# A hybrid attention and convolution layer on one core: the DRAM scratch of v and q laid out for two load transfers a head

## The chip, the core and the metric

The kernel runs on one core of a Trainium2 chip. A core has a matrix engine (TensorE, PE in the profile, its weight loads as PEld), a vector engine (VectorE, DVE), a scalar engine (ScalarE, ACT), GpSimd (POOL), an engine that here only issues transfers (SyncE, SP) and 16 DMA engines that move data between DRAM and the on-chip memory. Engines run side by side; each takes its own instructions in order and waits where data isn't there yet. A transfer is issued by an instruction in the queue of SP, ACT or POOL. The metric is the device time of one execution in microseconds (us); lower is better.

## The reference

One layer over 1024 latent tokens (16 rows of 64) of width 1024, with 256 context tokens.

```python
h  = rmsnorm(x, norm_g) * (1 + scale) + shift          # adaLN from c; hc likewise from ctx
q, k, v, za, u, bg, cg, zc = split(h @ w_in)           # 8 x 512 columns
kc, vc = split(hc @ w_in[:, 512:1536])
q, k, kc = rmsnorm per head (8 heads of 64)
s_lat = rope(q) . rope(k) / 8 + bias, in an 8 x 16 window; s_ctx = q . kc / 8
p = softmax over both;  attn = (p_lat . v + p_ctx . vc) * silu(za)
conv = bg * conv3(cg * u) * silu(zc)
out = x + gate * (concat(attn, conv) @ w_out)
```

Everything is float32. Products of full precision are made from a high and a low part of each factor, so q, k, v and the weights each exist twice.

## The kernel before

The work has four stages. First the conditioning, the normalised and transposed tokens and the first convolution group. Then the projections of q, k and v (the loop at line 1161): four pairs of heads, eight token tiles of 128 each. Then the attention (line 1284): 8 heads in four quarters each, 32 quarters and a tail, with the matmuls of the remaining columns of `w_in` as fillers between a quarter's parts. Last the output projection (from line 1311).

On-chip memory doesn't hold q, k and v of all heads, so the projections write them to scratch in DRAM and the attention loads a head at a time.

- Writing: `spill` (203) keeps stores in a list that `flush` (1157) sends to SP's queue once per tile. `turn_qk` (226) writes, for two token tiles at a time, q (`q_d`, line 243: for each head a store for the high and one for the low part, each with rotated and plain q) and k (`k_d`). Line 1209 writes v of two token tiles (`v_d`), `turn_kc` (269) the context's k and v (`kc_d`, `vc_d`, 279 and 280).
- Reading, class `head` (927): `load_k` (935) two transfers of 512 KB; `load_q` (941) four of 256 KB for q, two of 128 KB for the context's k; `load_v` (951) for high and low part four of 64 KB, each with two blocks of v, and one of 64 KB with the context's two blocks, ten in all; `masks` (960) one of 576 KB with the bias. In DRAM `q_d` is [high or low, 64, pair of tiles, rotated or plain, 256] and `v_d` [128, pair of tiles, high or low, 128]. On the chip v of a head is `[128, 2, 10, 65]`: eight blocks of v and two of the context, 64 columns each and a column that sums the weights; there are two such tiles (`vts`, 1249), and head h uses the one of head h - 2.

The order in the attention: PE, DVE, ACT and POOL keep the program's order (class `ordered`, 44; `strict`, 1279). SP is not among them there, so the scheduler places its transfers, and neither are the transfers that ACT issues: `ordered` leaves `dma_start` of the other engines alone. The loop (1284) asks for v of head h at its first quarter, for bias, q and the context's k of head h + 1 at its second and for k of head h + 1 at its third.

A quarter n (`quarter`, 1057) does the scores of two blocks (`scores`, 983, into `pss`) and of 256 queries against the context (`ctx_scores`, into `pc`, copied to `sc` by ACT), the maxima (`mx`, then transposed on PE as `pmx`, reduced to `rm`, spread and copied by ACT to `mg`) and exponentials (`phc`, `plc`, `phl`, `pll`) of quarter n - 2, and the products with v (`ctx_out`, `lat_out`, into `po`) of quarter n - 3. In `finish` (1029) ACT copies half a finished head to `ob` and issues two stores from its own queue, the sums (`rs_d`, 1033) and the output (`o_d`, 1034). The fillers load their weights as `uraw` (`unit_load`, 291, on SP) and ACT casts them to `uh`; each filler unit's SiLU is stored to `zs_d` (495) by SP. `gated` (1257) multiplies finished pairs with that.

```python
        def put():
            ...
                for l in range(2):
                    spill(q_d[h][l, :, t0 // 2], qs[rows, l])
    ...
    def load_v(self):
        ...
        for l in range(2):
            for t in range(4):
                sp.dma_start(self.v[:, l, 2 * t:2 * t + 2, 0:HD]..., v_d[h][:, t, l]...)
            sp.dma_start(self.v[:, l, NB:, 0:HD]..., vc_d[h][:, l]...)
```

Of the kernel before, what the change touches and what calls it, by code (L numbers as in the profile page):

```python
# [10 lines left out]
F32 = mybir.dt.float32  # L11
# [8 lines left out]
P = 128  # L20
D = 1024
T = 1024
# [3 lines left out]
NB = 8  # L26
NH, HD = 8, 64
# [12 lines left out]
def body(tc, es, x, ctxt, w_ada, b_ada, w_in, q_g, k_g, rpbr, w_out, vecs, cst, out):  # L40
# [22 lines left out]
    sp = ordered(nc.sync)  # L63
# [26 lines left out]
    def many(name, n, shape):  # L90
        return [dr.tile(shape, F32, name=f"{name}{i}")[:] for i in range(n)]
# [9 lines left out]
    zs_d = many("zs_d", NPAIR, [P, T])  # L101


    q_d = many("q_d", NH, [2, HD, 4, 2, 256])
    k_d = many("k_d", NH, [HD, 4, 2, 256])
    v_d = many("v_d", NH, [P, 4, 2, 2 * HD])
    kc_d = many("kc_d", NH, [HD, 2, L])
    vc_d = many("vc_d", NH, [P, 2, 2 * HD])
    ri_d = many("ri_d", NPAIR, [2, T])


# [48 lines left out]
    def chunk_load(col, k):  # L160
        raw = wpp.tile([P, 3, P], F32, name="wr", tag="wr", bufs=5)
        chunk_anchor[:] = [sp.dma_start(raw, bass.AP(w_in.tensor, w_in.offset + (k * P) * 4096 + col,
                                                     [[4096, P], [512, 3], [1, P]]))]
        return raw
# [23 lines left out]
    def halves(dst, lo, src):  # L188
        act.copy(dst, src)
        dve.tensor_tensor(lo, src, dst.bitcast(F32), ALU.subtract)  # L190

    def put_v(vs, i, ps):

        halves(vs[:, :, 0, i], vs[:, :, 1, i], ps.rearrange("p (s d) -> p s d", s=2))
# [8 lines left out]
    def spill(dst, src):  # L203
        stores.append(lambda: sp.dma_start(dst, src.bitcast(F32)))
# [21 lines left out]
    def turn_qk(pp, p, two, t0):  # L226

        pA = psm.tile([P, 2, 2, P], F32, name="trA", tag="C", bufs=2)
        pB = psm.tile([P, 512], F32, name="trB", tag="C", bufs=2)
        for i, (qn, rot) in enumerate(two):  # L230
            pe.transpose(pA[:, 0, i], rot[:, 0:P], ident)
            pe.transpose(pA[:, 1, i], qn[:, 0:P], ident)
            pe.transpose(pB[:, i * P:(i + 1) * P], rot[:, P:256], ident)

        def put():
            qs = pp.tile([P, 2, 2, 256], F32R, name="qs", tag="qs", bufs=2)
            halves(qs[:, 0], qs[:, 1], pA[:].rearrange("p k i d -> p k (i d)"))
            ks = pp.tile([P, 2, 256], F32R, name="ks", tag="ks", bufs=2)
            halves(ks[:, 0], ks[:, 1], pB[:, :256])
            for s in range(2):  # L240
                h, rows = 2 * p + s, slice(64 * s, 64 * s + 64)
                for l in range(2):
                    spill(q_d[h][l, :, t0 // 2], qs[rows, l])
                spill(k_d[h][:, t0 // 2], ks[rows])
        return put

# [22 lines left out]
    def turn_kc(pp, p, two, vs):  # L269
        pB = psm.tile([P, 512], F32, name="trC", tag="C", bufs=2)  # L270
        for i in range(2):
            pe.transpose(pB[:, i * P:(i + 1) * P], two[i], ident)

        def put():
            ks = pp.tile([P, 2, 256], F32R, name="ks", tag="ks", bufs=2)
            halves(ks[:, 0], ks[:, 1], pB[:, :256])
            for s in range(2):
                h, rows = 2 * p + s, slice(64 * s, 64 * s + 64)
                spill(kc_d[h], ks[rows])
                spill(vc_d[h], vs[:, s].rearrange("p l i d -> p l (i d)"))  # L280
        return put

    def proj_tile(ch, t):
        ps = bank("pacc", "OOSS"[t % 4])
        for k in range(KT):
            wh, wl = ch[k]
            mm3(ps[:, :384], hh[k][:, t * P:(t + 1) * P], hl[k][:, t * P:(t + 1) * P], wh, wl, k == 0, k == KT - 1)
        return ps


    def unit_load(col):
        raws = []
        for q in range(2):
            raws.append(uw.tile([P, 4, P], F32, name="uraw", tag="uraw", bufs=2))
            sp.dma_start(raws[q], w_in[0, q * 512:(q + 1) * 512, col:col + P].rearrange("(k p) n -> p k n", p=P))
        return raws
# [84 lines left out]
    def z_col(f):  # L381
        return CZA + f * P if f < 4 else CZC + (f - 4) * P
# [407 lines left out]
    for m in range(1, 4):  # L790
        k, new, last = 2 * m, m < 3, m == 3
# [135 lines left out]
    class head:  # L927
# [13 lines left out]
        def load_q(self):  # L941
            h = self.h
            self.q = self.place().tile([P, 2, T], F32R, name="q_s", tag="B")
            self.kc = bmp.tile([P, 2, L], F32R, name="kc_s", tag="kc_s", bufs=2)
            for i in range(2):
                rows = slice(64 * i, 64 * i + 64)
                for k in range(2):
                    sp.dma_start(self.q[rows, k].bitcast(F32).rearrange("p (t c) -> p t c", c=256), q_d[h][i, :, :, k])
                sp.dma_start(self.kc[rows].bitcast(F32), kc_d[h])

        def load_v(self):
            h = self.h
            self.v = vts[h % 2]
            for l in range(2):
                for t in range(4):
                    sp.dma_start(self.v[:, l, 2 * t:2 * t + 2, 0:HD].bitcast(F32),
                                 v_d[h][:, t, l].rearrange("p (b d) -> p b d", d=HD))
                sp.dma_start(self.v[:, l, NB:, 0:HD].bitcast(F32), vc_d[h][:, l].rearrange("p (b d) -> p b d", d=HD))

        def masks(self):  # L960
            self.bt = bmp.tile([P, 3, 384], F32, name="bt", tag="bt", bufs=2)
# [195 lines left out]
    def flush():  # L1157
        while stores:
            stores.pop(0)()

    for n in range(NT + 3):


        p, t = divmod(n, NB)
        at = 2 if p < NPAIR - 1 else 0
        if 1 <= t and p + 1 < NPAIR:
            raws += [chunk_load(CQ + (p + 1) * P, k) for k in ([t - 1] if t < NB - 1 else [t - 1, t])]
        if n == 0:
            loaded[z_col(4)] = unit_load(z_col(4))
        if n == NT - 8:  # L1170
            loaded[z_col(0)] = unit_load(z_col(0))
        if 1 <= n <= KT:
            gate.load(n - 1)
        if 9 <= n < 25 and n % 2:
            next(tables)
        if n == NT - 6:
            heads[0].masks()
            heads[0].load_k()
        if n == NT - 5:
            heads[0].load_q()  # L1180
        flush()

        if t == 0 and 0 < n < NT:
            nxt += map(chunk_split, raws)
            ch, nxt, raws = nxt, [], []
        if n == 0:
            next(group0)
        if n == NT - 4:
            next(fill)
        if n < NT:  # L1190
            tiles[n] = proj_tile(ch, t)
        else:
            for _ in range((4, 3, 1)[n - NT]):
                next(fill)
        if 5 <= n < 9:
            for _ in range(2):
                next(group0)
        if n == 9:
            for _ in group0:
                pass  # L1200
        if 0 < n <= NT:
            scales[n - 1] = head_scale(pp, tiles[n - 1], 4)
            if n % 2:
                vs = pp.tile([P, 2, 2, 2, HD], F32R, name="vs", tag="vs", bufs=4)
            put_v(vs, (n - 1) % 2, tiles[n - 1][:, 256:384])
            if n % 2 == 0:
                q, r = divmod(n - 1, NB)
                for s in range(2):
                    spill(v_d[2 * q + s][:, r // 2], vs[:, s].rearrange("p l i d -> p l (i d)"))
        if t == at + 1 and n < NT:  # L1210
            cscales = [head_scale(pp, a, 2) for a in cacc]

        if 1 < n <= NT + 1:
            m, r = n - 2, (n - 2) % NB
            qn = rms_normed(pp, tiles[m], scales.pop(m))
        while waiting:
            waiting.pop(0)()
        if 4 <= t and p + 1 < NPAIR:
            nxt.append(chunk_split(raws.pop(0)))
        if 1 < n <= NT + 1:  # L1220
            tiles[m] = rotated(pp, rope, qn, r)
        if t == at + 2 and n < NT:
            kc = normed_ctx(pp, cacc, cscales)
        do_dves()
        if 2 <= n < KT + 2:
            gate.add(n - 2)
        if 9 <= n < 25 and n % 2 == 0:
            next(tables)
        do_acts()

        if n == KT + 5:
            gate.sum()
        if t == at and n < NT:
            cacc = ctx_products(ch)
        if n % 2 == 0 and n >= 4:
            waiting.append(turn_qk(pp, (n - 4) // NB, [tiles.pop(n - 4), tiles.pop(n - 3)], (n - 4) % NB))
        if t == at + 3 and n < NT:
            waiting.append(turn_kc(pp, p, *kc))
# [38 lines left out]
    with sbuf("att") as ap, psum("psb") as psb:  # L1277
# [6 lines left out]
        for n in range(4 * NH + 4):  # L1284
            h, g = divmod(n, 4)
# [7 lines left out]
            if ready:  # L1293
                p = ready.pop()
# [138 lines left out]
```

## Time and profile before

| | us |
|---|---|
| median of 3 runs | 649.57 (648.65 to 651.94) |
| the profiled execution | 650.83 |
| its span, first to last instruction | 649.0 |

The span is shorter than the execution because what lies before the first and after the last instruction is not in it. Busy times in the profile are sums of what an engine executed; issuing a transfer and waiting are not counted as busy. Matmuls overlap, and their ends are modelled, so a PE that is busy throughout may still be a little under its peak. A row of a timeline has start, duration, engine, line, operation, the tiles written and read, and in brackets how long the engine had idled before it and what ended that. Many groups show L55, the line of the helper that keeps the order; they are told apart by their tiles.

### The profile page before, as it was taken

The page shows a single profiled execution, that of the slowest core. Times are in us where ns is not written, and L with a number is a line of the kernel's source. Part 1 is how long each engine was busy: PE and PEld are TensorE (multiplying, and loading weights), DVE is VectorE, ACT ScalarE, POOL GpSimd, SP SyncE. Part 2 cuts the span into 40 slices and gives each one's busy share as a digit, 9 for nine tenths or more (in the row PEclk, how much of TensorE's full clock was granted, in tenths as well). Part 3 has the DMA queues.
Part 4 walks back from the last instruction along what each step waited for, and adds up shares of the span by engine and source line. Part 5 has one row for each costly group of instructions (what it writes and reads, how often), then busy time and mean ns, then how long its engine had stood idle before and what let it go on. Part 6 is the DMA issues. An engine that isn't in the chain of part 4 may idle for free.

```text
span 649.0 us, 10300 instructions
## 1 busy us (share of the span) xinstructions
PE 631.6 (97%) x3482; PEld 542.1 (84%) x3482; DVE 431.1 (66%) x814; ACT 322.6 (50%) x693; POOL 130.1 (20%) x138
## 2 busy tenths in 40 slices
PE   7999999999999999999998999999999999999997
PEld 2577899999899999877787888888888888888885
DVE  1576756865775846458786789988998864575111
ACT  4566735533534544448676558565685644352000
POOL 2105003313223231102111111111211111004421
PEclk9799999999999999999999999999999999999999
DMA  8972656768694999799847677886862223865521
GB/s 322 321 250 97 166 177 197 212 223 232 214 288 139 270 269 237 196 238 216 215 126 195 152 171 195 208 213 155 229 168 75 74 77 115 310 236 204 197 102 49
DMA packets 118864, 125.46 MB, mean 193 GB/s; under 512 B 32817, under 2 KB 89353, under 8 KB 117532
## 3 DMA queue, kind: packets, MB, share of 16 engines
q1 hardware_dynamic: 112348, 113.23, 60.6%
q10 hardware_dynamic: 6208, 11.05, 5.4%
q8 instruction: 27, 0.44, 0.3%
q0 software_dynamic: 256, 0.54, 0.3%
q14 instruction: 25, 0.20, 0.1%
HBM read 88.01 MB, written 38.53 MB: 195 GB/s over the span
## 4 chain that ended last, share of the span: by engine, by line
PE 71%; DMA 9%; DVE 7%; ACT 5%; SPq 4%; issue 2%; POOL 1%; ACTq 0%; DVEq 0%
PE pu L55 20%; PE pacc L55 17%; PE po L55 5%; PE pout L76 4%; PE pout L75 4%; PE pout L74 4%; DMA k_s<-k_d 3%; SPq L55 3%; PE tr L55 3%; PE cacc L55 3%; PE pss L55 2%; PE acc L55 2%; PE pmx L55 2%; DVE mx L55 2%; DMA v<-v_d 2%
## 5 line engine op out<-in xcount | busy, mean ns | idle before, releaser
L55 PE MATMUL pu<-h,uh 128*128 128x512 f32 x544 | 169.0, 392 | 0.0
L55 PE MATMUL pacc<-wh,h 128*128 128x384 f32 x512 | 135.2, 338 | 0.0
L55 PEld LDWEIGHTS pu<-h,uh 128*128 128x128 f32 x544 | 98.2, 188 | 17.1
L55 PE MATMUL pu<-h,ul 128*128 128x512 f32 x272 | 106.3, 391 | 0.0
L55 PEld LDWEIGHTS pacc<-wh,h 128*128 128x128 f32 x512 | 92.8, 188 | 0.1
L55 POOL TENSOR_TENSOR plc<-sc,phc 128x512 fp32r<-128x512 f32 x32 | 42.7, 1335 | 224.1 <-ACT sc L55 88.5
L55 PE MATMUL pacc<-wl,h 128*128 128x384 f32 x256 | 85.6, 334 | 0.0
L55 POOL TENSOR_TENSOR ss<-ss,few 128x4 f32<-128x4 f32 (+1 forms) x40 | 42.0, 1051 | 127.1 <-DVE ss L55 126.7
L55 PEld LDWEIGHTS pu<-h,ul 128*128 128x128 f32 x272 | 51.1, 188 | 11.2
L55 DVE TENSOR_TENSOR mx<-mx,sb 128x384 f32<-128x384 f32 (+1 forms) x64 | 54.8, 864 | 2.0
L75 PE MATMUL pout<-wol,yh 128*128 128x512 f32 x128 | 49.8, 389 | 0.0
L76 PE MATMUL pout<-woh,yl 128*128 128x512 f32 x128 | 49.6, 389 | 0.0
L74 PE MATMUL pout<-woh,yh 128*128 128x512 f32 x128 | 48.3, 389 | 0.0
L55 PEld LDWEIGHTS pacc<-wl,h 128*128 128x128 f32 x256 | 48.1, 188 | 0.1
L55 DVE TENSOR_REDUCE ss<-sq 128x4 f32<-128x260 f32 (+1 forms) x40 | 15.7, 393 | 46.2 <-ACT sq L55 45.2
L55 ACT COPY mg<-pmx 128x256 f32<-128x256 f32 x32 | 12.0, 374 | 61.2 <-PE pmx L55 46.7
L55 ACT ACTIVATE sq<-pacc 128x256 f32<-128x256 f32 x32 | 12.3, 386 | 52.8 <-PE pacc L55 51.9
L1365 DVE TENSOR_TENSOR ot<-pout,gate 128x512 f32<-128x512 f32 x16 | 10.8, 687 | 38.6 <-PE pout L76 36.3
L55 DVE TENSOR_TENSOR pll<-sb,phl 128x768 fp32r<-128x768 f32 (+2 forms) x33 | 29.3, 889 | 8.9 <-ACT sb L55 8.9
L55 DVE TENSOR_TENSOR sc<-sc,mg 128x512 f32<-128x512 f32 x32 | 21.8, 682 | 18.4 <-ACT mg L55 18.4
L1366 POOL TENSOR_TENSOR ot<-ot,xr 128x512 f32<-128x512 f32 x15 | 20.1, 1347 | 68.2 <-DVE ot L1365 66.0
L55 ACT ACTIVATE qn<-pacc,ss 128x64 f32<-128x64 f32 x128 | 30.1, 330 | 6.5 <-POOL ss L55 3.2
(149 smaller groups left out, 1281.5 us busy)
## 6 DMA issues: line engine op xcount, KB each, us to landing
uraw<-in_w_in SPq DMA_DIRECT2D x34, 256.0 KB
q_d<-qs SPq DMA_DIRECT2D x64, 128.0 KB
k_s<-k_d SPq DMA_DIRECT2D x16, 512.0 KB
q_s<-q_d SPq DMA_DIRECT2D x32, 256.0 KB
wr<-in_w_in SPq DMA_DIRECT2D x40, 192.0 KB
slab<-in_w_ada SPq DMA_DIRECT2D x6, 1024.0 KB
t_d<-btw SPq DMA_DIRECT2D x8, 576.0 KB
bt<-t_d SPq DMA_DIRECT2D x8, 576.0 KB
```

What stands on the lines that cost most here:

```text
L55: i = emit(*a, **kw)
L74: i = pe.matmul(ps, ah, bh, start=first, stop=False)
L75: pe.matmul(ps, ah, bl, start=False, stop=False)
L76: pe.matmul(ps, al, bh, start=False, stop=last)
L1365: dve.tensor_tensor(ot, ps, gate[:, cols], ALU.mult)
L1366: (dve if (nh, t) == (1, NB - 1) else pool).tensor_tensor(ot, ot, xr, ALU.add)
```

## The change

The scratch of v and q is laid out in the order in which the attention reads it. `v_d` of a head becomes [128, high or low, 10 x 64], and takes the context's v as its last two blocks, so that `vc_d` goes; `q_d` becomes [high or low, 64, rotated or plain, 1024]. `load_v` then has one transfer for the high and one for the low part, `load_q` one for each. The stores stay as many; a store of q now writes two runs of 1 KB per row in place of one of 2 KB, a store of v two runs of 512 bytes in place of one of 1 KB.

```diff
-    q_d = many("q_d", NH, [2, HD, 4, 2, 256])
+    q_d = many("q_d", NH, [2, HD, 2, T])
     k_d = many("k_d", NH, [HD, 4, 2, 256])
-    v_d = many("v_d", NH, [P, 4, 2, 2 * HD])
+    v_d = many("v_d", NH, [P, 2, (NB + 2) * HD])
     kc_d = many("kc_d", NH, [HD, 2, L])
-    vc_d = many("vc_d", NH, [P, 2, 2 * HD])
@@ turn_qk
-                    spill(q_d[h][l, :, t0 // 2], qs[rows, l])
+                    spill(q_d[h][l, :, :, t0 * P:t0 * P + 256], qs[rows, l])
@@ turn_kc
-                spill(vc_d[h], vs[:, s].rearrange("p l i d -> p l (i d)"))
+                spill(v_d[h][:, :, NB * HD:], vs[:, s].rearrange("p l i d -> p l (i d)"))
@@ load_q
-                for k in range(2):
-                    sp.dma_start(self.q[rows, k].bitcast(F32).rearrange("p (t c) -> p t c", c=256), q_d[h][i, :, :, k])
+                sp.dma_start(self.q[rows].bitcast(F32), q_d[h][i])
@@ load_v
-                for t in range(4):
-                    sp.dma_start(self.v[:, l, 2 * t:2 * t + 2, 0:HD].bitcast(F32),
-                                 v_d[h][:, t, l].rearrange("p (b d) -> p b d", d=HD))
-                sp.dma_start(self.v[:, l, NB:, 0:HD].bitcast(F32), vc_d[h][:, l].rearrange("p (b d) -> p b d", d=HD))
+                sp.dma_start(self.v[:, l, :, 0:HD].bitcast(F32), v_d[h][:, l].rearrange("p (b d) -> p b d", d=HD))
@@ the projections' loop
-                    spill(v_d[2 * q + s][:, r // 2], vs[:, s].rearrange("p l i d -> p l (i d)"))
+                    spill(v_d[2 * q + s][:, :, (r - 1) * HD:(r + 1) * HD], vs[:, s].rearrange("p l i d -> p l (i d)"))
```

## Prediction

> **What bounds the kernel now.** I read the page first, then busy time by stage, then what the matrix engine waits for, then the chain of waits, and last the queues of ACT and SP beside each other. The page's busy line:
>
> ```profile
> PE 631.6 (97%) x3482; PEld 542.1 (84%) x3482; DVE 431.1 (66%) x814; ACT 322.6 (50%) x693; POOL 130.1 (20%) x138
> ```
>
> PE is the bound: 631.6 of 649.0 us. Only the rest can be won without taking matmuls away. Busy time by stage says where it lies (stretch, its length, then busy time of PE, PEld, DVE, ACT, POOL with counts, granted clock, share of the DMA engines, GB/s):
>
> ```profile
> 110.00:270.00 160.00, 159.02 (x964) 153.66 (x965) 106.80 (x290) 71.46 (x268) 42.38 (x48) 1.00 0.79 229
> 270.00:360.00 90.00, 84.20 (x459) 69.85 (x459) 64.33 (x103) 55.65 (x94) 12.17 (x11) 0.98 0.79 195
> 360.00:550.00 190.00, 189.71 (x1078) 161.25 (x1077) 160.47 (x246) 116.71 (x193) 32.09 (x29) 1.00 0.58 152
> ```
>
> The projections (110 to 270 us) leave PE 1.0 us idle, the later attention (360 to 550) 0.3 us. The first quarters of the attention, 270 to 360, leave 5.8 us idle, and there alone the clock is under full. The change acts on transfers written in the first of these stages and read in the other two. Within the middle one:
>
> ```profile
> 320.00:330.00 10.00, 9.24 (x52) 7.52 (x50) 8.36 (x13) 6.98 (x11) 2.86 (x2) 1.00 0.35 90
> ```
>
> ```profile
> 340.00:350.00 10.00, 9.83 (x61) 8.37 (x60) 5.17 (x8) 5.19 (x7) 1.30 (x1) 1.00 0.97 262
> 350.00:360.00 10.00, 8.29 (x39) 7.07 (x38) 8.27 (x13) 5.41 (x11) 1.27 (x1) 0.83 0.45 118
> ```
>
> The last row matters most: 1.71 us idle, and a clock of 0.83 over 10 us, which is 1.7 us of clock lost. What PE waited for between 264 and 550 us (total, times, longest):
>
> ```profile
> PE pmx L55 <- DVE mx L55: 2.8, 5, 1.5
> PE pmx L55 <- DVE rm L55: 1.2, 5, 0.5
> PE pc L55 <- DVE qs L55: 1.1, 1, 1.1
> PE po L55 <- POOL plc L55: 0.6, 1, 0.6
> ```
>
> No transfer is among them: no matmul has waited for a load of q, k or v. So fewer loads are worth nothing by themselves. The chain of waits, though, has two transfers of the changed region on it:
>
> ```profile
> 307.54 10.82 DMA v<-v_d
> ```
>
> ```profile
> 338.61 11.54 DMA k_s<-k_d
> ```
>
> They end at 318.36 and 350.15 us. ACT's queue in order of time shows who was waiting:
>
> ```profile
> 314.92 0.49 ACTq L1033 DMA_DIRECT2D rs_d<-ob  x1
> 316.20 1.09 ACT L55 ACTIVATE zs<-pu 128x512 f32<-128x512 f32 x2
> 318.39 0.51 ACTq L1034 DMA_DIRECT2D o_d<-ob  x1
> 318.99 0.37 ACT L55 COPY mg<-pmx 128x256 f32<-128x256 f32 x1 [1.71 <-DMA v<-v_d]
> ```
>
> ```profile
> 348.45 0.21 ACTq L1033 DMA_DIRECT2D rs_d<-ob  x1
> 350.17 0.45 ACTq L1034 DMA_DIRECT2D o_d<-ob  x1
> 350.72 0.37 ACT L55 COPY mg<-pmx 128x256 f32<-128x256 f32 x1 [4.74 <-PE po L55]
> ```
>
> The store of a finished head (L1034) goes out 0.02 us after a load has landed that it has nothing to do with. ACT was free at 317.28 and at 345.98 (318.99 less 1.71, 350.72 less 4.74), and everything that follows in its queue stood behind the store. The second label names PE, but the store at 350.17 is what stands in between. Why that load? SP's queue at the same time:
>
> ```profile
> 302.95 2.70 SPq L948 DMA_DIRECT2D q_s<-q_d  x4
> 305.74 0.54 SPq L962 DMA_DIRECT2D bt<-t_d  x1
> 306.34 1.10 SPq L939 DMA_DIRECT2D k_s<-k_d  x2
> 307.54 1.41 SPq L956 DMA_DIRECT2D v<-v_d  x2
> 309.87 1.97 SPq L295 DMA_DIRECT2D uraw<-in_w_in  x2
> 312.82 1.81 SPq L956 DMA_DIRECT2D v<-v_d  x2
> 318.25 0.81 SPq L495 DMA_DIRECT2D zs_d<-zs  x2
> ```
>
> ```profile
> 333.43 3.44 SPq L948 DMA_DIRECT2D q_s<-q_d  x4
> 336.98 0.54 SPq L962 DMA_DIRECT2D bt<-t_d  x1
> 337.62 0.38 SPq L295 DMA_DIRECT2D uraw<-in_w_in  x1
> 338.05 1.89 SPq L939 DMA_DIRECT2D k_s<-k_d  x2
> 340.03 1.36 SPq L495 DMA_DIRECT2D zs_d<-zs  x2
> 341.49 5.89 SPq L956 DMA_DIRECT2D v<-v_d  x4
> ```
>
> Count back from the store at 350.17 over SP and ACT together: rs_d 1, v 2 to 5, zs_d 6 and 7, second half of k_s (issued at 338.61) 8. From the store at 318.39: first zs_d 1, rs_d 2, v 3 and 4, uraw 5 and 6, v 7, and the v piece of 307.54 is 8. Both times the releaser is the eighth transfer back. I take it as this program's rule: no transfer is issued before the eighth ahead of it, on either queue, has landed. Eight slots, and v pieces of 64 KB fill them as fast as halves of k of 512 KB.
>
> **The change part by part.**
>
> Loads. Per head, v and context v go from ten issues to two and q from four to two: 80 issues fewer over eight heads. By the SP rows two v issues take 1.41 us and four q issues 2.70, so 64 x 0.7 + 16 x 0.68 is about 56 us of SP's time, stalls included. SP feeds PE nothing that PE waits for, so this counts zero; its bounds are in the range with the rest of the idle time below.
>
> Slots, which is the term that pays. Take the v pieces out of the two sequences. From the store at 318.39: zs_d, rs_d, uraw 2, k_s 2, bt, second q half is the eighth. It is ahead of bt and k (by the code's shapes 0.59 and 1.05 MB) in the queue; the v piece behind them landed at 318.36; at the stage's 195 GB/s over a share of 0.79, 247 GB/s, 1.64 MB take 6.6 us, so q is in by about 311.7, 5.6 us before ACT is free. From the store at 350.17: rs_d, zs_d 2, k_s 2, uraw, bt, second q half again. Behind it come bt, uraw and k, 1.90 MB, 7.2 us at the 262 GB/s of the 340 to 350 row, so it has landed by 342.9, 3.1 us before ACT is free at 345.98. The order may slip by one or two and still find bt or uraw, in by 345.1 and 346.1. So neither store waits.
>
> What that is worth, from PE's side. First, at 350 to 360: PE's last wait there and what stands behind it:
>
> ```profile
> 355.18 0.30 PE L55 MATMUL pmx<-ci,mx 128*128 128x128 f32 x1 [1.51 <-DVE mx L55]
> 355.68 0.33 PE L55 MATMUL pmx<-ci,mx 128*128 128x128 f32 x1 [0.20 <-DVE mx L55]
> 355.78 0.65 PE L55 MATMUL po<-phc,v 128*65 128x256 f32 x2
> ```
>
> DVE's mx comes out of the sequence that starts with ACT's mg at 350.72. With mg up to 4.2 us earlier (345.98 to 350.17), all of the 1.71 us goes: 1.7, bounds 0 and 1.71. Second, the clock: it fell right behind this gap and is full in the other stretches where PE idles under 1 us, so it goes with it: 1.7, bounds 0 and 1.7. Third, at 320 to 330: mg up to 1.7 us earlier, idle 0.76; part of it is ACT's other work, so 0.7, bounds 0 and 0.76. ACT's waits before stores after 360 are worth nothing: that stage has 0.3 us to give. The remaining idle time of 270 to 360, 5.80 - 1.71 - 0.76 = 3.3 us, I leave where it is (ACT and DVE work between two matmuls); its bound is 0 to 3.3. Sum: 1.7 + 1.7 + 0.7 = 4.1 us.
>
> The v load waits longer. A transfer may now go only when all blocks of the head two before it are read, and its reader waits for the whole; behind it in SP's queue stand the next kc, uraw and q loads. At 328.81 the last two pieces of head 2 go out:
>
> ```profile
> 328.81 0.88 SPq L956 DMA_DIRECT2D v<-v_d  x2
> ```
>
> The first matmul that reads head 2's v is the po of 355.78, 26 us later. The new pair is 0.66 MB: 2.5 us at 262 GB/s, 2.7 at 247. Cost zero; what hides it is three quarters of matmuls, and if they were gone it would be those 2.7 us a head. Its issue, ten pieces a partition in one instruction, has no row; between one issue of the row above (0.44) and all five it replaces (2.2), I take 0.44 since an issue of four v pieces or four q rows has about the same time each; SP has the room.
>
> Stores. q_d takes 64 stores and v_d 40 as before, of the same 13.6 MB, but in pieces half as long. At worst their rate falls from the projections' 290 GB/s (229 over 0.79) to the 247 of the next stage: 55.1 - 46.9 = 8.2 us of transfer time over 160 us, in which the DMA engines idle 0.21 x 160 = 34. PE is 159.02 of 160 busy there. Cost zero, bounds 0 and the 1.0 us that PE already idles there, doubled.
>
> From the profiled execution, 650.83 us around a span of 649.0: 646.7. That execution lies 1.3 over the median of the runs, 649.57; the same 4.1 from the median give **645.5 us**.
>
> **The rivals.**
>
> *The clock does not follow.* The fall to 0.83 stands once in this stretch, behind a gap of 1.51 us; one instance doesn't show that the gap made it. If it belongs to the sparse stretch as a whole, or was not in the median run, the clock term goes and the gain is 1.7 + 0.7 = 2.4 us: 647.2. For it speaks that the stage's other gaps, of 0.2 to 0.6 us, left the clock full; against it, that the gap which goes is the longest of the stage. Chance 0.2. The Trainium skill, "TensorE: Matmul & The Clock Gate", Part 1, says that the clock is halved after an idle window of about 3.4 us and that this window runs freely. By that rule a gap of 1.5 us need not halve it, and the time would be the 647.2 of this rival; the 1.7 us lost here would be one such window at half speed, with which the row agrees in size, while its gap is too short for the rule.
>
> *Another transfer takes the eighth place.* In the attention SP's order is not chained by hand, so other transfers may slide to where a store finds a half of k again; or a large transfer is cut up on its way and the count does not fall. Then nothing goes: 649.6. Against: the order has to slip by three places. Chance 0.16.
>
> *SP stands behind v.* Two rows on the queue, of SP and of ACT (total, times, longest):
>
> ```profile
> SPq L956 <- PE po L55: 11.6, 9, 2.7
> ```
>
> ```profile
> ACT uh L55 <- DMA uraw<-in_w_in: 4.5, 2, 2.9
> ```
>
> SP issues in order. A v pair put into its queue a quarter too early blocks the uraw, kc and q loads behind it, and ACT, which casts uraw in program order, waits. A quarter is 7.9 us (k_s of one head at 306.34, of the next at 338.05, a fourth of it). ACT's 4.74 us cost 3.4; 7.9 would cost 5.7, in two heads before 360 11.4, less the 4.1: 656.9. It decides once the pair stands more than some 3 us ahead of its release, since 2.7 costs nothing visible today. Chance 0.12.
>
> **How the numbers follow.** Forecast 0.52, clock stays 0.2, another transfer 0.16, SP behind v 0.12. A measurement of this kernel tells about 0.5% from no change, 3.2 us, so faster means under 646.3 and slower over 652.8. The forecast lies under that line by 0.8 us, so a little of it falls within: faster 0.5, same 0.38, slower 0.12. The range goes from all idle time and clock of 270 to 360 won (5.8 + 1.7: 642.1) to the no-gain case at the highest run before (651.9); only the slower rival is left out.
>
> **What would show it.** Right: sixteen v loads and sixteen q loads on SP, ACT's mg after L1034 with an idle time under 1 us around 318 and 350, PE's idle time in 270 to 360 near 3.4 us, clock 1.00 there. Wrong: a store of L1034 still released by a k or v landing; PE waiting for q or v; SP waiting at the v load for PE po by over 3 us with uraw late on ACT; a clock under 1 without a gap. What would break the whole argument is a gap of the same size made by something ACT does anyway.

## The result, and the profile after

The changed kernel is slower: 659.18 us median (655.91 to 661.41, four runs), the kernel before on the same chip 649.17 (648.65 to 651.94); ratio 1.0146, 95% interval 1.0116 to 1.0175. The forecast was 645.5 us, with a range up to 651.9. The profiled execution took 655.91 us around a span of 654.1, 5.1 us more than the 650.83 of before. It is the shortest of the four, and what it lost is about half of what the medians differ by.

Busy time first, from the page, and then by stage (columns as in the prediction):

```profile
PE 632.9 (97%) x3482; PEld 541.4 (83%) x3482; DVE 431.8 (66%) x814; ACT 322.5 (49%) x693; POOL 131.0 (20%) x138
```

```profile
0.00:110.00 110.00, 104.01 (x559) 78.80 (x559) 61.56 (x119) 58.19 (x103) 19.33 (x29) 0.95 0.65 214
...
270.00:360.00 90.00, 84.90 (x474) 70.93 (x473) 64.63 (x103) 57.08 (x96) 12.05 (x11) 1.00 0.79 195
360.00:550.00 190.00, 185.99 (x1055) 156.88 (x1054) 157.73 (x241) 115.06 (x190) 31.67 (x28) 1.00 0.60 152
```

Two things are to be seen. From 270 to 360 us PE gained 0.7 us of busy time and the clock is full (0.98 before). From 360 to 550, a stage with 0.3 us of idle time before, PE is now idle for 4.0. The first row is a stage that the change doesn't touch: the clock there was 0.95 in this execution and 0.97 in that of before. That matters for the 5.1 us. At the first matmul `pu<-h,uh` (115.55 us before, 117.86 after) the changed kernel is already 2.3 us behind; at the last `po` (542.27 and 546.76) it is 4.5 behind. So what the change touches took 2.2 us longer in this execution, the difference of a gain and a larger loss.

Within these stages the forecast gain and the new loss can be told apart. Before the change 290 to 300 had 9.89 us of PE, and 410 to 420 and 480 to 490 had 10.00 each:

```profile
350.00:360.00 10.00, 10.00 (x57) 8.71 (x58) 8.24 (x13) 6.08 (x12) 1.57 (x1) 1.00 0.49 140
```

```profile
290.00:300.00 10.00, 8.32 (x46) 6.89 (x45) 6.38 (x10) 7.89 (x14) 1.26 (x1) 1.00 0.79 231
410.00:420.00 10.00, 8.04 (x44) 6.46 (x43) 9.86 (x16) 6.30 (x11) 2.62 (x4) 1.00 0.56 170
480.00:490.00 10.00, 8.56 (x48) 6.94 (x47) 9.86 (x16) 8.96 (x14) 1.41 (x2) 1.00 0.35 109
```

At 350 the 1.71 us of idle time and the clock of 0.83 are gone, as forecast: 3.4 us. The other three rows together lost 1.6 + 2.0 + 1.4 = 5.0 us. Who waited is in the waits between 264 and 550 us (total, times, longest):

```profile
ACT uh L55 <- DMA uraw<-in_w_in: 10.3, 3, 6.1
PE pmx L55 <- DVE mx L55: 6.4, 10, 1.6
DVE zs L55 <- DMA zs<-zs_d: 4.8, 2, 3.2
...
DVE tb L55 <- DMA tb<-o_d: 1.4, 1, 1.4
```

PE still waits for no load. But the loads that ACT and DVE wait for are later: uraw (4.5 us before, 10.3 now), and zs and tb, which stood in no row before.

The longest of these waits is at 290 us, where uraw is late because SP issues it late, at 287.51 us (281.20 before). In SP's queue ahead of it, q and k of head 1 (2 MB) now go out from 271.88 us on, and behind them two stores of q, 1.2 us elsewhere, hold SP for 5.12:

```profile
276.07 5.12 SPq L55 DMA_DIRECT2D q_d<-qs  x2
287.51 0.38 SPq L294 DMA_DIRECT2D uraw<-in_w_in  x1
```

```profile
291.19 0.62 ACT L55 CAST uh<-uraw 128x512 fp32r<-128x512 f32 x1 [6.09 <-DMA uraw<-in_w_in]
```

The worst place after 360 us on SP's queue, with DVE's, ACT's and PE's timelines behind it:

```profile
395.27 1.12 SPq L946 DMA_DIRECT2D q_s<-q_d  x2
396.44 0.59 SPq L938 DMA_DIRECT2D k_s<-k_d  x1
397.13 0.53 SPq L1270 DMA_DIRECT2D y_d<-tb  x1
397.70 0.74 SPq L1263 DMA_DIRECT2D zs<-zs_d  x1
```

```profile
407.22 0.69 DVE L55 TENSOR_TENSOR zs<-zs,rb 128x512 f32<-128x512 f32 x1 [3.17 <-DMA zs<-zs_d]
```

```profile
408.55 0.63 ACT L55 ACTIVATE phc<-sc 128x512 fp32r<-128x512 f32 x1 [2.88 <-DVE sc L55]
```

```profile
411.81 0.30 PE L55 MATMUL pmx<-ci,mx 128*128 128x128 f32 x1 [1.58 <-DVE mx L55]
```

zs, 256 KB, is issued behind two halves of q and one of k, 1.5 MB. DVE, which works in order, stands 3.17 us before its product; everything behind it in the quarter (sc, the exponentials on ACT, mx, pmx on PE) slides with it. From 390 to 480 us the chain of waits has this load, the tb load and three stores on it (start, us):

```profile
393.18 2.95 DMA o_d<-ob
397.70 9.49 DMA zs<-zs_d
457.93 2.67 DMA rs_d<-ob
461.12 6.24 DMA y_d<-tb
467.44 11.31 DMA tb<-o_d
```

tb is late in two steps: its one buffer is free only when the store of y_d has landed (467.36), and the load issued then takes 11.31 us.

Before, the chain had v and k on it, behind which ACT's stores stood. Those stores now go at once: in ACT's timeline the output (third row) is issued 0.25 us after the sums (second row), and these as soon as the copy of ob is done:

```profile
348.43 0.56 ACT L55 COPY ob<-po 65x512 f32<-65x512 f32 x1
349.03 0.21 ACTq L1028 DMA_DIRECT2D rs_d<-ob  x1
349.28 0.45 ACTq L1029 DMA_DIRECT2D o_d<-ob  x1
350.38 0.37 ACT L55 COPY mg<-pmx 128x256 f32<-128x256 f32 x1 [1.38 <-PE pmx L55]
```

### The profile page after: what moved, and what is told of

Its sections match the earlier page's. It is cut to its first block, busy times and chain, and to the rows that moved or that the text cites. A ratio compares the mean times of both kernels' runs of the same rounds, so it can differ in the third digit from the quotient of the medians.

```text
span 654.1 us, 10160 instructions
## 1 busy us (share of the span) xinstructions
PE 632.9 (97%) x3482; PEld 541.4 (83%) x3482; DVE 431.8 (66%) x814; ACT 322.5 (49%) x693; POOL 131.0 (20%) x138
## 4 chain that ended last, share of the span: by engine, by line
PE 67%; DMA 12%; DVE 8%; ACT 5%; SPq 4%; issue 2%; POOL 1%; ACTq 0%; DVEq 0%; POOLq 0%
PE pu L55 20%; PE pacc L55 17%; PE po L55 5%; SPq L55 4%; PE pout L76 3%; PE pout L74 3%; PE pout L75 3%; PE tr L55 3%; PE cacc L55 3%; PE pss L55 2%; PE acc L55 2%; DMA tb<-y_d 2%; PE pmx L55 2%; DMA tb<-o_d 2%; DVE mx L55 2%
## 5 line engine op out<-in xcount | busy, mean ns | idle before, releaser
L55 DVE TENSOR_TENSOR mx<-mx,sb 128x384 f32<-128x384 f32 (+1 forms) x64 | 56.4, 890 | 2.0
L55 ACT CAST uh<-uraw 128x512 fp32r<-128x512 f32 x34 | 20.7, 619 | 23.7 <-DMA uraw<-in_w_in 23.6
```

Source lines behind the costliest of these rows:

```text
L55: i = emit(*a, **kw)
```

## The experiments

All ratios are to the kernel before on the same chip, with their 95% intervals. The theories named in the expectations: 'order' (SP's order puts a whole head's q and k early), 'size' and 'slots' (larger transfers in eight places cost by themselves), 'layout' (the new stores or pieces in DRAM cost), 'runs' (pieces of 8 KB cost), and from the ninth experiment on 'ahead' (what counts is how many bytes stand on SP ahead of a small load that somebody waits for).

### v in two transfers, q as before

```diff
 # against the changed kernel
-    q_d = many("q_d", NH, [2, HD, 2, T])
+    q_d = many("q_d", NH, [2, HD, 4, 2, 256])
-                sp.dma_start(self.q[rows].bitcast(F32), q_d[h][i])
+                for k in range(2):
+                    sp.dma_start(self.q[rows, k]..., q_d[h][i, :, :, k])
```

> Only v is changed (layout, stores and two loads a head); q stays as before. Theory 'order': with v in two pieces the scheduler puts q and k of head 1 (2 MB) on SP's queue ahead of the last stores and of the uraw loads, and the zs and tb loads of the finished pairs behind q and k; ACT and DVE, which keep the program's order, then wait. This kernel has that early q and k too, so 654 to 660 us, with ACT waiting for uraw by 4 us or more near 285 us. Theory 'size': larger transfers in the eight slots put more bytes ahead of every small one, whatever the order; two thirds of the removed issues are here, so 654 to 657. Theory 'layout': stores in half-length runs slow the transfers; v has 40 of 104 such stores, so 652 to 654.

Measured: 647.22 us (645.84 to 648.38), ratio 0.9961 [0.9942, 0.998]. All three theories had expected 652 us or more; the v half is faster than before. By stage:

```profile
270.00:360.00 90.00, 86.64 (x486) 72.50 (x485) 66.62 (x105) 59.62 (x100) 13.38 (x12) 1.00 0.77 197
...
360.00:550.00 190.00, 189.72 (x1075) 161.13 (x1074) 160.27 (x246) 114.92 (x190) 32.77 (x32) 1.00 0.61 158
```

86.64 us against 84.20, at full clock, and nothing lost after 360: the forecast term, alone.

### q in two transfers, v in ten as before

```diff
 # against the changed kernel
-    v_d = many("v_d", NH, [P, 2, (NB + 2) * HD])
+    v_d = many("v_d", NH, [P, 4, 2, 2 * HD])
+    vc_d = many("vc_d", NH, [P, 2, 2 * HD])
 # load_v and the stores of v as in the kernel before
```

> Only q is changed (layout, stores and two loads a head); v stays in ten loads. In this kernel the scheduler leaves q and k of head 1 behind the uraw loads, as before the change. Theory 'order': 647 to 652 us, no uraw wait on ACT near 285 us over 2 us. Theory 'size': q halves of 512 KB in the slots, a third of the effect, 651 to 654. Theory 'layout': 64 of 104 stores have shorter runs, 653 to 657.

Measured: 661.35 us, ratio 1.0169 [1.0131, 1.0207], above what any of the three theories had expected. The q half alone is as slow as the whole change, though not in the same way: here the late zs and, since v is still in ten pieces, stores of ACT behind k and v stand side by side, and the wait for uraw near 285 us is only 1.8 us:

```profile
DVE zs L55 <- DMA zs<-zs_d: 5.5, 2, 4.8
ACT mg L55 <- DMA k_s<-k_d: 5.2, 1, 5.2
...
ACT mg L55 <- DMA v<-v_d: 4.0, 1, 4.0
```

### The layouts and stores, but ten and four loads

```diff
 # against the changed kernel
-                sp.dma_start(self.q[rows].bitcast(F32), q_d[h][i])
+                for k in range(2):
+                    sp.dma_start(self.q[rows, k].bitcast(F32), q_d[h][i, :, k])
-                sp.dma_start(self.v[:, l, :, 0:HD]..., v_d[h][:, l]...)
+                for t in range(5):
+                    sp.dma_start(self.v[:, l, 2 * t:2 * t + 2, 0:HD]..., v_d[h][:, l, 2 * t * HD:(2 * t + 2) * HD]...)
```

> The new layouts of q_d and v_d and all their stores, but loads in ten and four pieces as before. Order on SP is nearly that of before. Theories 'order' and 'size': 647 to 651 us. Theory 'layout': 656 to 661, like the changed kernel.

Measured: 651.23 us, ratio 1.0021 [0.9993, 1.0049]. That is just above the 647 to 651 of the two other theories and far under the 656 of 'layout', which falls: stores in half-length runs cost at most the 0.5% that the interval leaves room for.

### SP in the program's order

```diff
-        strict[:] = every
+        strict[:] = every + [sp]
```

> The changed kernel with SP's transfers held to the program's order in the attention too, so that uraw comes ahead of the q and k loads that the program asks for later. Theory 'order': 643 to 650 us, no uraw wait over 2 us near 285 us, though zs and tb still stand behind q and k of their quarter, and a store that waits for its data may now hold up loads behind it. Theory 'size': 655 to 661, since slots and sizes are those of the changed kernel.

Measured: 652.87 us, ratio 1.0057 [1.002, 1.0093], in neither theory's range: about half of the way from the changed kernel (1.0146) to v alone (0.9961), so SP's order matters. But the program's order makes a wait of its own (ACT's for uraw, 14.6 us in all), and v alone had already been fast with q and k of head 1 as early as in the changed kernel. 'order' as I had put it falls: the early start by itself isn't what costs.

### q in four, with long pieces

```diff
-                sp.dma_start(self.q[rows].bitcast(F32), q_d[h][i])
+                for k in range(2):
+                    sp.dma_start(self.q[64 * i + 32 * k:64 * i + 32 * k + 32]..., q_d[h][i, 32 * k:32 * k + 32])
```

> The changed kernel with q in four transfers of 32 partitions instead of two of 64; pieces of 8 KB in DRAM as in the changed kernel. Theory 'slots' (at most eight transfers of SP and ACT are under way; with q in two of them rather than four, the transfers that follow are let go with more bytes still ahead of them, so zs, tb and uraw land late): 645-650 us, like v in two with q in four short ones (647.2); zs no longer waits for its load by over 1.5 us. Theory 'runs' (pieces of 8 KB hold the DMA engines longer, so that other transfers' pieces come late): 655-662 us, as changed.

Measured: 649.76 us (646.03 to 655.17), ratio 1.0021 [0.9988, 1.0055]: most of the loss is gone with pieces of 8 KB, though the executions spread more than those of the other kernels near 650 us. SP's order has all four quarters of q, 1 MB, ahead of zs here, and DVE waits for zs for 1.95 us, where 'slots' had expected under 1.5:

```profile
393.49 1.91 SPq L947 DMA_DIRECT2D q_s<-q_d  x4
395.49 0.37 SPq L1271 DMA_DIRECT2D y_d<-tb  x1
395.91 0.43 SPq L1264 DMA_DIRECT2D zs<-zs_d  x1
```

### q in two, with pieces of 1 KB

```diff
-    q_d = many("q_d", NH, [2, HD, 2, T])
+    q_d = many("q_d", NH, [2, HD, 2, 4, 272])
-                sp.dma_start(self.q[rows].bitcast(F32), q_d[h][i])
+                sp.dma_start(self.q[rows]....rearrange("p k (t c) -> p (k t) c", c=256),
+                             q_d[h][i].rearrange("p k t c -> p (k t) c")[:, :, 0:256])
```

> The changed kernel with q in two transfers whose pieces in DRAM are 1 KB as before (a gap of 64 bytes behind each 1 KB). Theory 'slots': 655-662 us, as changed, with DVE waiting for zs's load by over 2 us. Theory 'runs': 645-650 us.

Measured: 662.15 us, ratio 1.0211 [1.0162, 1.026], no faster than with long pieces. Together the two runs, long pieces without most of the loss and short pieces with all of it, rule 'runs' out.

### Both layouts, v in two, q in four

```diff
-                sp.dma_start(self.q[rows].bitcast(F32), q_d[h][i])
+                for k in range(2):
+                    sp.dma_start(self.q[rows, k].bitcast(F32), q_d[h][i, :, k])
```

> The changed kernel's layout and its v in two, q in four transfers (each with pieces of 4 KB). Theory 'slots': 645-650 us. Theory 'runs': between, 649-655 us. It is also the candidate for the best version: both layouts, only q's number of transfers as before.

Measured: 646.74 us (646.43 to 648.62), ratio 0.9969 [0.995, 0.9988], with a span of 644.8 us in the profile: the fastest median of all runs, 0.3% under the kernel before. Its SP queue where the changed kernel's was worst:

```profile
391.58 1.84 SPq L947 DMA_DIRECT2D q_s<-q_d  x3
393.52 0.53 SPq L1271 DMA_DIRECT2D y_d<-tb  x1
394.09 0.43 SPq L1264 DMA_DIRECT2D zs<-zs_d  x1
394.56 0.48 SPq L947 DMA_DIRECT2D q_s<-q_d  x1
395.09 0.60 SPq L938 DMA_DIRECT2D k_s<-k_d  x1
```

Three quarters of q, 0.75 MB, stand ahead of zs, and DVE doesn't wait for it.

### Two more of the eight places taken

```diff
-            sp.dma_start(self.bt[:].rearrange("p v n -> p (v n)"), t4_d[self.h])
+            for v in range(3):
+                sp.dma_start(self.bt[:, v], t4_d[self.h][:, v * 384:(v + 1) * 384])
```

> The changed kernel with the table bt of a head loaded in three transfers instead of one: the same bytes and the same order on SP, two more of the eight places taken per head. Theory 'slots': part of the loss comes back, 648-655 us. Theory 'runs': nothing, 655-662 us. If 'slots' holds and it gets slower instead, it is because the smaller loads now meet a half of k at the eighth place.

Measured: 660.3 us, ratio 1.0171 [1.0129, 1.0214]: nothing came back. It speaks against 'slots' only in part, for at 400 us bt stands behind zs in SP's queue, where its places hold nothing back that zs could gain from.

### k held behind the small loads

```diff
 # unit_load and gated: small[:] = [the last load of uraw or tb]
-                sp.dma_start(self.k[64 * i:64 * i + 64].bitcast(F32), k_d[h])
+                put = sp.dma_start(self.k[64 * i:64 * i + 64].bitcast(F32), k_d[h])
+                if small:
+                    behind(put, small[0])
```

> The changed kernel, q in two, with one thing held: the two loads of a head's k are put on SP only behind the last uraw or tb load that the program has named before them. So uraw (around 285 us) and zs, tb (around 400 us) no longer stand behind k, with the number and the size of all transfers as in the changed kernel. Theory 'ahead' (what counts is how many bytes of q and k stand on SP ahead of a small load that DVE or ACT waits for; q in two lets SP's order put k in front of it): 645-652 us, DVE's wait for zs under 2.5 us and ACT's for uraw under 3.5 us. Theory 'slots' (the two larger pieces in eight places by themselves): 654-662 us, as changed.

Measured: 652.45 us (649.5 to 654.07), ratio 1.0041 [1.0018, 1.0064]. The transfers are those of the changed kernel, only k's place on SP is another, and over half of the way from the changed kernel (1.0146) to v alone (0.9961) is made. 'ahead' expected 645 to 652, so this is just past its upper end: DVE's wait for zs fell below 2.5 us, but ACT's for uraw stayed at 5.5 where 3.5 was expected, and tb is late:

```profile
ACT uh L55 <- DMA uraw<-in_w_in: 10.3, 2, 5.5
...
DVE zs L55 <- DMA zs<-zs_d: 2.7, 2, 2.0
DVE tb L55 <- DMA tb<-o_d: 2.0, 1, 2.0
```

The last has its reason in the edit: the load named last before head 7's k was uraw, so that k still went out ahead of tb there:

```profile
460.45 0.56 SPq L940 DMA_DIRECT2D k_s<-k_d  x1
464.12 0.33 SPq L1268 DMA_DIRECT2D tb<-o_d  x1
```

### k in four

```diff
-            for i in range(2):
-                sp.dma_start(self.k[64 * i:64 * i + 64].bitcast(F32), k_d[h])
+            for i in range(4):
+                sp.dma_start(self.k[32 * i:32 * i + 32]..., k_d[h][32 * (i % 2):32 * (i % 2) + 32])
```

> The changed kernel, q in two, with k in four transfers of 256 KB instead of two of 512 KB. Around 395 us SP's order then has q twice, a quarter of k, zs: 1.25 MB ahead of zs where the changed kernel has 1.5 MB and the kernel with q in four 0.75 MB. Theory 'ahead': between, 649-656 us, zs waiting some 1.5 to 3 us. Theory 'slots': k's two extra places hold back what q's two missing ones let go: 646-651 us.

Measured: 652.68 us, ratio 1.0045 [1.0018, 1.0072], where 'ahead' had it (649 to 656); 'slots' had 646 to 651. DVE's longest wait for zs is 2.2 us.

### zs and tb on POOL's queue

```diff
-            sp.dma_start(zs, zs_d[f][:, cols])
-            sp.dma_start(tb, o_d[f][:, cols])
+            pool.dma_start(zs, zs_d[f][:, cols])
+            pool.dma_start(tb, o_d[f][:, cols])
             load_sums(f, half, rb, sp)
```

> The changed kernel with zs, tb and rb of the gated heads loaded from POOL's queue instead of SP's. Theory 'ahead', if it is the place in SP's queue that counts: the waits for zs and tb go and with them the loss around 410 and 480 us, some 4 us; the late uraw around 290 us stays: 651-656 us. If it is the bytes under way on the DMA engines, whatever the queue: zs as late as before and 656-662 us.

The edit moves zs and tb; rb, which the expectation names too, stayed on SP.

Measured: 658.8 us, ratio 1.0138 [1.0083, 1.0194], as slow as changed. Of the transfers issued from 390 to 404 us (KB, us from issue to landing):

```profile
zs<-zs_d POOLq DMA_DIRECT2D x1, 256.0 KB, 9.4
```

POOL issues zs at 402.37 us, just behind the same 1.5 MB of q and k, which SP issues from 400.51 to 402.34. From POOL's queue zs lands after 9.4 us, from SP's in the changed kernel after 9.49. So at this place it isn't the position in one queue: the bytes under way hold zs up, whichever queue it comes from. The Trainium skill, "DMA: Bandwidth & Descriptors", Issuing engines are not separate DMA queues, says that transfers from any issuing engine end up on the same 16 DMA engines and interleave there; the two landing times agree. POOL also met waits of its own here (10.7 us for y_d ahead of tb), and ACT's wait for uraw grew to 16.1 us in all, so the time of this run doesn't show what a free queue would give.

### v in two, q in four, k in four

```diff
 # the edits of "v in two, q in four" and of "k in four" together
```

> Both new layouts, v in two, q in four and k in four too: still smaller pieces for what is large. Theory 'ahead': as with k in two (646.7) or up to 1 us better, 645-648 us, since no wait for a load is left there but ACT's for uraw. Theory 'slots': 645-648 us too. If the number of transfers by itself costs (SP's issue time), 648-652 us.

Measured: 646.99 us, ratio 0.9965 [0.9948, 0.9983]: no better than with k in two. PE's busy time in the two stages is that of k in two (86.66 and 189.72 us, there 86.65 and 189.72), so smaller pieces won nothing.

### q and k held behind the small loads

```diff
 # unit_load and gated: small["uraw"], small["tb"] = the last load of each
+    def held(put):
+        for i in small.values():
+            behind(put, i)
-                sp.dma_start(self.q[rows].bitcast(F32), q_d[h][i])
+                held(sp.dma_start(self.q[rows].bitcast(F32), q_d[h][i]))
 # and the loads of k likewise
```

> The changed kernel, q in two and k in two, with the loads of a head's q and k both put on SP behind the last uraw and the last tb load that the program has named before them, so that uraw (around 285 us), zs and tb (around 395 and 470 us) stand ahead of q and k. Number, size and pieces of all transfers are those of the changed kernel. Theory 'ahead': the whole loss goes, 645-650 us; no wait for zs or tb over 1 us. Theory 'slots': 653-662 us. If q or k of the next head comes too late for PE, a wait of PE for q_s or k_s shows, and 650-655 us.

Measured: 647.78 us (645.39 to 648.87), ratio 0.9971 [0.9945, 0.9997]. With q in two and k in two, every transfer as large as in the changed kernel, the whole loss is gone, as 'ahead' had it. This decides between 'ahead' and 'slots'. The queue and the stages:

```profile
395.69 0.42 SPq L1269 DMA_DIRECT2D zs<-zs_d  x1
397.36 0.32 SPq L1270 DMA_DIRECT2D tb<-o_d  x1
397.77 0.38 SPq L963 DMA_DIRECT2D bt<-t_d  x1
398.25 1.09 SPq L952 DMA_DIRECT2D q_s<-q_d  x2
```

```profile
270.00:360.00 90.00, 86.66 (x486) 72.55 (x485) 65.43 (x105) 58.49 (x98) 12.51 (x12) 1.00 0.79 197
360.00:550.00 190.00, 189.73 (x1075) 161.30 (x1074) 160.34 (x244) 115.63 (x192) 32.87 (x32) 1.00 0.60 157
```

zs and tb go first, q follows. No wait for zs or tb is left, and PE's stages are those of v alone (86.64 and 189.72). That q and k go out later costs nothing that shows.

### v in two, q in four, k held

```diff
 # "v in two, q in four", with held(...) around the loads of k
```

> v in two, q in four (646.7 us), with the loads of k behind the last uraw and tb load as well. Theory 'ahead': nothing small waits there now but uraw (3.5 us of ACT at its longest), so no change or up to 1 us better, 645.5-647.5 us.

Measured: 647.78 us, ratio 0.9972 [0.9949, 0.9995]: just above the range expected and no gain over the same without holding.

### The dose

The first load of zs after 390 us, by what SP has issued of q and k just ahead of it, and DVE's wait for it, from the timelines of each run:

| | MB ahead | DVE waits, us |
|---|---|---|
| q and k held | 0 | none |
| the kernel before, and all others with q in four but the one below | 0.75 | none |
| q in four, long pieces | 1.0 | 1.95 |
| k held, q in two | 1.0 | 0.66 |
| k in four | 1.25 | 2.21 |
| q in two, short pieces | 1.5 | 2.94 |
| the changed kernel | 1.5 | 3.17 |
| bt in three | 1.5 | 3.84 |
| q in two, v in ten | 1.5 | 4.83 |

The wait grows with the bytes ahead, but they aren't all of it: 1.0 MB gave 0.66 us with k held well behind zs and 1.95 with k issued right behind it, and 1.5 MB gave from 2.9 to 4.8.

## Why the prediction was wrong

- **Stores behind a load's landing: right.** The stores go at once (quoted above). The rule of eight is borne out: in the traces the transfers of SP and ACT (607 before, 527 after) signal their landing on eight semaphores, shared out evenly. And v alone brings a gain: 2.5 us in the medians (647.22 against 649.70) where 4.1 were forecast. In the profiled executions it is larger: the middle stage gained 2.44 us of PE's busy time (84.20 to 86.64), the clock went from 0.98 to 1.00, and from the first `pu<-h,uh` to the last `po` v alone takes 4.8 us less. The term was there; for the median it was over-sized, and 2.5 us is the price that the rival "the clock does not follow" had (2.4). One trace of before can't tell whether its half-clock spell is in most of its executions.
- **Loads: the step that failed.** "SP feeds PE nothing that PE waits for, so this counts zero." The zero was right for v, and in that PE still waits for no load. It left out the small loads that SP issues among those of q and that share the DMA engines with them: uraw for ACT, zs and tb for DVE, behind which PE then waits for DVE. For this term I had read the waits of PE alone; ACT's wait for uraw stood in a row that I quoted for a rival and did not price against q. With q in two, the order that the scheduler made for SP has 1.5 MB of q and k ahead of zs, with q in four 0.75 MB. That is 12 us between 659.18 and 647.22 (ratios 1.0146 and 0.9961), and holding q and k gives it back (0.9971, which the intervals don't tell from 0.9961) by moving the loads, with none of them resized.
- **The note on order: half seen.** "In the attention SP's order is not chained by hand, so other transfers may slide to where a store finds a half of k again". They did slide, but what they delayed was not a store.
- **SP stands behind v: didn't happen.** v in two is faster, and SP's waits at the v load for PE's po between 264 and 550 us fell from 11.6 to 4.1 us. The victim of that rival, uraw on ACT, was the right one at 290 us; its cause was q and k. At 656.9 us this rival was the only slower case priced, and the range left it out.
- **Layout and stores at zero: right** (651.23, ratio 1.0021 with 1 inside its interval).
- **Clock: right here, in part by luck.** The spell at 350 went with its gap. But a gap of 1.58 us at 411.81 in the changed kernel left the row of 410 to 420 at a clock of 1.00, so a gap of that length doesn't always bring one. Both executions run at half clock early on, until 24.80 us before and until 25.78 us in the changed kernel, and the spell at 355.89 begins 97 times 3.413 us after that. Rows cut at the spell's bounds (the first two, of before) and on the same grid in the changed kernel (the third) show the difference:

```profile
352.48:355.89 3.41, 1.70 (x9) 1.00 (x8) 3.34 (x6) 3.35 (x7) 1.27 (x1) 1.00 0.50 131
355.89:359.30 3.41, 3.41 (x16) 3.41 (x15) 2.95 (x6) 0.40 (x2) 0.00 (x0) 0.50 0.27 76
```

```profile
408.07:411.48 3.41, 2.16 (x10) 1.47 (x8) 3.38 (x5) 2.87 (x5) 1.27 (x1) 1.00 0.96 282
```

The clock was halved for 3.41 us, behind a stretch of 3.41 us in which PE was busy for 1.70. In the changed kernel the gap of 1.58 us fell across the bound of two such stretches, and the emptier has 2.16 us of PE. The 16 traces of this case have eleven such spells between that early one and 550 us, ten of 3.41 us and one of 6.83. Each begins on this grid, behind a stretch in which PE was busy for at most 0.52 of the time; three stretches with 0.46 to 0.57 had no spell behind them. So where a gap falls counts as well as its length, which the prediction had no term for. The Trainium skill, "TensorE: Matmul & The Clock Gate", Part 1, asks for an idle window of about 3.4 us; the full clock behind 1.58 us agrees with that, the 0.83 behind the 1.51 us of before does not.
- **Still open.** The profiled execution lost 5.1 us, the median 10, and no longer execution of the changed kernel has a trace. Two longer ones of other kernels with q in two have: q alone (662.99 us) and q in short pieces (661.85) lose 11.6 and 10.2 us between the first `pu<-h,uh` and the last `po`, where the changed kernel lost 2.2, with the same kinds of waits, longer (zs 4.8 us at most, uraw 9.6), and three and two spells of half clock. That the changed kernel's longer executions lost in this way is likely, not shown. At 290 us the loss goes with the order; holding k alone moved uraw's issue from 287.51 to 286.55 us and ACT's wait from 6.1 to 5.5, holding q and k moved it to 280.73 and left no wait at that place, so most of it is q's, as far as one trace of each shows.

## What to carry to other kernels

Before making loads larger, list for every engine the loads that it waits for, not only for the one that bounds, and count the bytes that are issued ahead of each of them. A transfer that nobody waits for is not free when it is large and goes out just ahead of a small one that somebody does wait for. If a scheduler sets the queue's order, merging transfers may change that order too; compare the two queues around each awaited load, and hold the large loads behind it.

## What the runs showed of the hardware

A 256 KB load behind 1.5 MB landed 9.49 us after its issue from SP's queue and 9.4 from POOL's: another queue did not carry it past the traffic. Shorter pieces did not help: q in two took 659.18 with pieces of 8 KB and 662.15 with pieces of 1 KB (ratios 1.0146 and 1.0211). And fewer, larger transfers were not better by themselves: v in transfers of 320 KB instead of 64 gained 0.4%, q in transfers of 512 KB instead of 256 lost 1.7% with v in ten and 2.1% with v in two and short pieces. The Trainium skill, "DMA: Bandwidth & Descriptors", Rules for kernel authors, advises to join many small transfers into a large one and names 64 KB as the size under which the overhead prevails; v, 64 KB before, did gain when joined, though what the traces show there is stores of ACT freed from waiting for the eighth transfer back and not an overhead of the small transfers; q, 256 KB before, lay above that size already.
